# Weight loads, casts and subtractions pinned to TensorE's order of use, and plain groups that multiply all high parts before the low parts

## The chip, the cores and the metric

The kernel runs on one core of a Trainium2 chip. The metric is the device time of one execution in microseconds, from the start of the program to its end. The time before is a median of three runs. Where a profile is quoted, it is of one profiled execution, and every time in it is counted from the first instruction of the span.

## The reference

One decoder layer on a sequence of 256 tokens, width 2048, all in float32: a SwiGLU half-step, a mixer (dilated attention beside gated linear attention), cross-attention into 256 memory tokens, and a second SwiGLU half-step. The change touches the two half-steps most:

```
def swiglu(h, w_gate, w_up, w_down):
    return (jax.nn.silu(h @ w_gate) * (h @ w_up)) @ w_down

x = x + 0.5 * swiglu(rms_norm(x, ffn1_norm), ffn1_w_gate, ffn1_w_up, ffn1_w_down)
x = x + hybrid_mixer(rms_norm(x, mix_norm), ...)
x = x + cross_attention(rms_norm(x, xattn_norm), ...)
x = x + 0.5 * swiglu(rms_norm(x, ffn2_norm), ffn2_w_gate, ffn2_w_up, ffn2_w_down)
```

`w_gate` and `w_up` are 2048 x 5632, `w_down` is 5632 x 2048; each half-step reads all three from HBM once.

## The kernel before

**Numbers in two parts.** TensorE multiplies in float32r, a shortened float32. To keep the accuracy every operand is split into a high part (`h`, the operand cast to float32r) and a low part (`l`, the rest): for a weight, ScalarE casts (`wh`, L136), VectorE subtracts (`wl`, L137). A product is then three matmuls: high by high, low of x by high of w, high of x by low of w.

**Tiles and loads.** A weight load is one DMA on SP's queue of 128 x 2048 values (1 MB), in tiles `raw`. In the half-steps there are six buffers for `raw`, three for `wh` and three for `wl`. A buffer is written again when its last reader is done: a `wh` or `wl` buffer when TensorE has finished its last matmul on it.

**A half-step.** The 5632 columns are eleven column blocks f of 512, in three parts (f 0 to 3, 4 to 7, 8 to 10). After each part its blocks go through `w_down`. Block 0 is done plainly (`proj`). From then on each f is one call of `strassen` for `w_gate` and `w_up` together, here called a pair; there are 10 in each half-step, 20 in all. A pair multiplies the first two groups of 512 rows by seven products, P1 to P7 (L194, 12 matmuls each), in place of eight, and the other two groups plainly, for gate and for up: G1 (gate, group 2), then P7, then G2 (up, group 2), G3 (gate, group 3), G4 (up, group 3), 24 matmuls each by `mm3` (L163 to L165). A matmul has 128 x 128 of x as stationary operand and 512 columns of weights moving.

**What stands around the products.** The four loads of a pair are `ral`, `rar`, `rbr`, `rbl`. P1 uses `ral`; then VectorE adds `rar` into `ral` (L212) for P2, and then `rbr` into `ral` (L212) for P3. POOL issues two DMAs that accumulate: `rbr` into `rar` for P5, and `rbl` into `ral` for P7 (L216). P1, P3, P5, P7, G1 and G3 write the PSUM tile `x`, P2 writes `y`. ScalarE copies P1's result from `x` to `c0l` (L228) before P3 writes `x` on, and `y` to `ys` (L234). VectorE makes `c0r = ys - x` after P3 (L238) and `c1r = ys - x` after P5 (L243); P5 and G1 write `x` on after these. At the end of a pair ScalarE makes `sg` of the gate (L377) and VectorE `h` (L385); `h` is transposed on TensorE after the next pair's P2 (L355), and split again (`hTh`, `hTl`, L274 and L275).

**What sets the order.** A scheduler orders each engine's instructions when the kernel is built, by priorities and by its own model of when operands are ready; weight loads, casts and subtractions have a raised priority. Each engine, SP's queue too, then works through its list in that order. On all engines, TensorE too, instructions can so stand in another order than they are written.

Of the kernel before, what the change touches and what calls it, by code (L numbers as in the profile page):

```python
# [8 lines left out]
F32 = mybir.dt.float32  # L9
# [9 lines left out]
TT = S // P  # L19
# [30 lines left out]
def layer_kernel(ctx: ExitStack, tc: tile.TileContext, A: dict, out: bass.AP):  # L50
    nc = tc.nc
    V, SC, G, PE, SY = nc.vector, nc.scalar, nc.gpsimd, nc.tensor, nc.sync
# [21 lines left out]
    def FT(tag, bufs, shape, dt, name):  # L74
        return phase["pool"].tile(shape, dt, tag=tag, name=name, bufs=bufs)

    def W2(shape, name, dt=F32):
        return sp.tile(shape, dt, tag="w", name=name)
# [4 lines left out]
    def PM(shape, name):  # L83
        return pm.tile(shape, F32, tag="ps", name=name)
# [7 lines left out]
    def tick():  # L92
        due = []
        for e in pend:
            e[0] -= 1
            if e[0] <= 0:
                due.append(e)
        for e in due:
            pend.remove(e)
            e[1]()  # L100


    gain = con.tile([P, 82], F32, name="gain")

    xload, wload = [], []
    open_phase("half1", True)
    with tc.high_priority(100000):
        SY.dma_start(gain, A["gains"])
        for g in range(3):
            raw = wp.tile([P, 4, 512], F32, tag="raw", name="raw")  # L110
# [10 lines left out]
    def load(W, c, g):  # L121

        if wload:
            return wload.pop(0)
        kn, n = W.shape[-2:]
        with tc.high_priority(WPRI):
            phase["loads"] += 1
            if phase["half_step"] and phase["loads"] % 2:
                raw = FT("raw", FRAW, [P, kn, n], F32, "raw")
            else:  # L130
                raw = wp.tile([P, kn, n], F32, tag="raw", name="raw")
            SY.dma_start(raw, W[c, g])
        return raw

    def split(wh, wl, src):
        SC.copy(wh, src)  # L136
        V.tensor_sub(wl, src, wh.bitcast(F32))  # L137

    def wgroup(W, c, g, fine=None):

        raw = load(W, c, g)
        n = W.shape[-1]
        kn = W.shape[-2]
        whole = phase["half_step"]
        m = kn if whole else kn // 2
        for h in range(1 if whole else 2):
            with tc.high_priority(WPRI):
                wh, wl = (FT(x, FWB if whole else WB, [P, m, n], F32R, x) for x in ("wh", "wl"))
                for i in range(m if fine else 1):
                    d = slice(i, i + 1) if fine else slice(0, m)  # L150
                    if fine:
                        fine(m * h + i)
                    split(wh[:, d], wl[:, d], raw[:, m * h + d.start:m * h + d.stop])
            ks = [(kn * g + m * h + kk, wh[:, kk], wl[:, kk]) for kk in range(m)]
            for i in range(0, m, kn // 2):
                yield ks[i:i + kn // 2]

    def mm3(acc, lhs, half, first, last, ts=range(TT), seeded=False):

        for t in ts:  # L160
            for i, (k, wh, wl) in enumerate(half):
                lh, ll = lhs(k, t)
                PE.matmul(acc[t], lh, wh, start=first and i == 0, stop=False, skip_group_check=seeded)  # L163
                PE.matmul(acc[t], lh, wl, start=False, stop=False, skip_group_check=seeded)  # L164
                PE.matmul(acc[t], ll, wh, start=False, stop=last and i == len(half) - 1, skip_group_check=seeded)  # L165

# [4 lines left out]
    def sums_of(ga, gb, put):  # L173

        (ah, al), (bh, bl) = ga, gb
        fa, fb = (FT("h", 8, [P, 4, S], F32, n) for n in ("fa", "fb"))
        V.tensor_add(fa, ah.bitcast(F32), al.bitcast(F32))
        V.tensor_add(fb, bh.bitcast(F32), bl.bitcast(F32))
        t0, t1 = slice(0, P), slice(P, S)
        sa, sb = (FT("h", 8, [P, 2, 4, P], F32, n) for n in ("sa", "sb"))  # L180
        V.tensor_sub(sa[:, 0], fa[:, :, t1], fb[:, :, t1])
        V.tensor_sub(sa[:, 1], sa[:, 0], fa[:, :, t0])
        V.tensor_sub(sb[:, 0], fa[:, :, t0], fa[:, :, t1])
        V.tensor_add(sb[:, 1], fb[:, :, t0], sa[:, 1])
        for i, x in enumerate((sa, sb)):
            split(*put(i), x)

    def product(acc, lhs, w, start):

        wh, wl = w  # L190
        first = start
        for i, j, w in ((0, 0, wh), (1, 0, wh), (0, 1, wl)):
            for k in range(4):
                PE.matmul(acc, lhs(k)[i], w[:, k], start=first, stop=j == 1 and k == 3, skip_group_check=not start)  # L194
                first = False
        tick()

    def strassen(Wl, cl, Wr, cr, lhs, ab, sums, groups):

        a, b = ab  # L200
        ral, rar = load(Wl, cl, a), load(Wr, cr, a)
        rbr, rbl = load(Wr, cr, b), load(Wl, cl, b)

        def parts(src):
            with tc.high_priority(WPRI):
                wh, wl = (FT(x, FWB, [P, 4, 512], F32R, x) for x in ("wh", "wl"))
                split(wh, wl, src)
            return wh, wl

        def add(dst, x, y):  # L210
            with tc.high_priority(WPRI):
                V.tensor_add(dst, x, y)  # L212

        def accumulate(dst, x):
            with tc.high_priority(WPRI):
                G.dma_start(dst, x, accum_op=ALU.add)  # L216

        def of(g, t):
            return lambda k: lhs(4 * g + k, t)

        def s_(i):
            return lambda k: tuple(x[:, i, k] for x in sums)

        x, y = PM([P, 512], "x"), PM([P, 512], "y")
        c0l, c0r, c1r = (pa.tile([P, 512], F32, tag="acc", name="acc") for _ in range(3))
        product(x, of(a, 0), parts(ral), True)
        with tc.high_priority(WPRI):
            SC.copy(c0l, x)  # L228
        add(ral, ral, rar)
        accumulate(rar, rbr)  # L230
        product(y, s_(0), parts(ral), True)
        with tc.high_priority(WPRI):
            ys = W2([P, 512], "ys")
            SC.copy(ys, y)  # L234
        add(ral, ral, rbr)
        product(x, s_(1), parts(ral), False)
        with tc.high_priority(WPRI):
            V.tensor_sub(c0r, ys, x)  # L238
        product(c0l, of(b, 0), parts(rbl), False)
        accumulate(ral, rbl)  # L240
        product(x, s_(2), parts(rar), False)
        with tc.high_priority(WPRI):
            V.tensor_sub(c1r, ys, x)  # L243
        product(c0r, s_(3), parts(rbr), False)
        accs = ((c0l, x), (c0r, c1r))
        for i, g in enumerate(groups):
            for acc, W, c in zip(accs, (Wl, Wr), (cl, cr)):
                for h, half in enumerate(wgroup(W, c, g)):
                    mm3(acc, lhs, half, False, i == len(groups) - 1 and h == 1, seeded=True)
                    tick()  # L250
                if i == 0 and W is Wl and c == cl:
                    product(x, of(b, 1), parts(ral), False)
        return accs

    def proj(W, c, lhs, groups, fine=None, last=False):

        n = W.shape[-1]
        acc = [pa.tile([P, n], F32, tag="acc", name="acc") for _ in range(TT)]
        groups = list(groups)
        for i, g in enumerate(groups):  # L260
            if fine and i:
                fine(4 * i)
            if last and i == len(groups) - 1:
                both = [w for half in wgroup(W, c, g) for w in half]
                for t in range(TT):
                    mm3(acc, lhs, both, i == 0, True, (t,))
                break
            for h, half in enumerate(wgroup(W, c, g, fine if i == 0 else None)):
                mm3(acc, lhs, half, i == 0 and h == 0, i == len(groups) - 1 and h == 1)
                tick()  # L270
        return acc
# [376 lines left out]
    for p2 in range(2):  # L648
        acc = proj(win, 8 + p2, lhs_x, range(4))
# [18 lines left out]
    for p2 in range(2):  # L668
        acc = proj(win, 10 + p2, lhs_x, range(4))
# [183 lines left out]
    acc = proj(A["xattn_w_k"], 0, lhs_mem, range(4))  # L853
# [6 lines left out]
    for c in range(NC):  # L860
        acc = proj(A["w_out"], c, lhs_m, (2, 3, 0, 1))
# [7 lines left out]
    acc = proj(A["xattn_w_q"], 0, lhs_x, range(4))  # L869
# [49 lines left out]
    for hv in range(2):  # L919
        acc = proj(A["xattn_w_v"], hv, lhs_mem, range(2))  # L920
# [7 lines left out]
    for c in range(0, NC, 2):  # L928
        pair = (c, c + 1)
        acc = {d: [pa.tile([P, 512], F32, tag="acc", name="acc") for _ in range(TT)] for d in pair}  # L930
# [104 lines left out]
```

## Time and profile before

| | |
|---|---|
| median of 3 runs | 1958.37 us (1956.77 to 1959.21) |
| the profiled execution | 1957.9 us |
| its span, first to last instruction | 1956.1 us |
| TensorE (PE) busy | 1924.5 us |
| VectorE (DVE) busy | 1270.5 us |
| ScalarE (ACT) busy | 988.7 us |
| read from HBM | 370.72 MB |

The profile names an instruction by engine, line and tiles (`wl<-raw,wh`: written from). A row of a timeline has the start, the time from the first start to the last end of equal instructions in a row, and in brackets how long the engine stood idle before and what it waited for. Matmuls overlap: one lasts 0.39 us in the profile, while the next starts long before that. The granted clock is the share of TensorE's full 2.4 GHz; its lower level, 0.5, is 1.2 GHz.

### The profile page before, as it was taken

How to read it: one execution, taken by the hardware profiler on the slowest of the kernel's cores; microseconds unless marked ns; L12 is line 12 of the kernel's file. 1: busy time of each engine (PE TensorE's matmuls, PEld its weight loads, DVE VectorE, ACT ScalarE, POOL GpSimd, SP SyncE). 2: the span in 40 equal slices, each digit the busy share in tenths (PEclk: the TensorE clock that was granted, in tenths of full speed). 3: DMA queues.
4: the chain of work that ended last, by engine and by line, in shares of the span. 5: the costliest groups of instructions: out<-in, count | busy, mean ns of one | idle time of the engine just before them, and what ended most of it. 6: DMA issues, size and time to landing. Idle time of an engine off the chain costs nothing.

```text
span 1956.1 us, 21465 instructions
## 1 busy us (share of the span) xinstructions
PE 1924.5 (98%) x8760; PEld 1586.4 (81%) x8760; DVE 1270.5 (65%) x1027; ACT 988.7 (51%) x956; POOL 96.1 (5%) x101
## 2 busy tenths in 40 slices
PE   8999999999999999999999999899999999999999
PEld 6888878888878888778888889688887788887887
DVE  6776467775578655546785566777646777457863
ACT  6555345553356446444675446555534555335642
POOL 2000000000000000002230000000000000000000
PEclk9999999999999999999999999999999999999999
DMA  9677547775567725445465554567755777556771
GB/s 368 235 236 258 190 148 264 271 268 192 173 220 237 281 82 186 156 167 191 172 232 207 183 192 151 217 236 233 260 184 146 252 272 274 203 178 215 237 285 59
DMA packets 63294, 416.14 MB, mean 213 GB/s; under 512 B 7099, under 2 KB 8251, under 8 KB 14428
## 3 DMA queue, kind: packets, MB, share of 16 engines
q1 hardware_dynamic: 56284, 370.74, 49.9%
q0 software_dynamic: 5760, 41.95, 10.4%
q10 hardware_dynamic: 1152, 2.10, 0.3%
q8 instruction: 68, 1.11, 0.2%
q14 instruction: 30, 0.25, 0.0%
HBM read 370.72 MB, written 2.10 MB: 191 GB/s over the span
## 4 chain that ended last, share of the span: by engine, by line
PE 74%; DVE 15%; ACT 5%; issue 4%; DMA 1%; POOL 0%; SPq 0%; ACTq 0%; DVEq 0%
PE acc L164 21%; PE acc L165 20%; PE acc L163 20%; DVE wl L137 10%; ACT wh L136 5%; PE x L194 4%; DVE raw L212 4%; PE x L165 1%; PE x L164 1%; PE acc L194 1%; PE x L163 1%; DVE h L385 1%; DMA xr<-in_xT_dram 1%; DVE acc L238 1%; PE y L194 0%
## 5 line engine op out<-in xcount | busy, mean ns | idle before, releaser
L137 DVE TENSOR_TENSOR wl<-raw,wh 128x2048 fp32r<-128x2048 f32 (+2 forms) x487 | 931.5, 1932 | 582.6 <-ACT wh L136 581.8
L136 ACT CAST wh<-raw 128x2048 fp32r<-128x2048 f32 (+2 forms) x487 | 777.0, 1619 | 692.5 <-PE acc L165 503.9
L163 PE MATMUL acc<-wh,xTh 128*128 128x512 f32 x1024 | 402.3, 394 | 16.3 <-ACT wh L136 16.3
L164 PE MATMUL acc<-wl,xTh 128*128 128x512 f32 x1024 | 402.9, 393 | 8.9 <-DVE wl L137 8.9
L165 PE MATMUL acc<-wh,xTl 128*128 128x512 f32 x1024 | 400.5, 391 | 0.0
L163 PE MATMUL acc<-wh,hTh 128*128 128x512 f32 x704 | 274.7, 390 | 0.0
L165 PE MATMUL acc<-wh,hTl 128*128 128x512 f32 x704 | 274.0, 389 | 0.0
L164 PE MATMUL acc<-wl,hTh 128*128 128x512 f32 x704 | 273.9, 389 | 0.0
L163 PEld LDWEIGHTS acc<-wh,xTh 128*128 128x128 f32 x1024 | 192.4, 189 | 59.5 <-ACT wh L136 18.9
L164 PEld LDWEIGHTS acc<-wl,xTh 128*128 128x128 f32 x1024 | 193.3, 189 | 56.9 <-DVE wl L137 17.7
L165 PEld LDWEIGHTS acc<-wh,xTl 128*128 128x128 f32 x1024 | 193.4, 189 | 39.7
L165 PEld LDWEIGHTS acc<-wh,hTl 128*128 128x128 f32 x704 | 132.2, 188 | 27.4
L164 PEld LDWEIGHTS acc<-wl,hTh 128*128 128x128 f32 x704 | 132.2, 188 | 27.2
L163 PEld LDWEIGHTS acc<-wh,hTh 128*128 128x128 f32 x704 | 132.2, 188 | 27.1
L216 POOL DMA_DIRECT2D raw<-raw x40 | 34.6, 864 | 1179.5 <-DVE raw L212 966.9
L212 DVE TENSOR_TENSOR raw<-raw 128x2048 f32<-128x2048 f32 x40 | 91.5, 2288 | 0.7
L165 PE MATMUL x<-wh,xTl 128*128 128x512 f32 x160 | 62.6, 391 | 0.0
L164 PE MATMUL x<-wl,xTh 128*128 128x512 f32 x160 | 62.5, 391 | 0.0
L163 PE MATMUL x<-wh,xTh 128*128 128x512 f32 x160 | 62.4, 390 | 0.0
L228 ACT COPY acc<-x 128x512 f32<-128x512 f32 x20 | 11.4, 571 | 95.6 <-PE x L194 95.6
L396 DVE SCALAR_TENSOR_TENSOR x<-acc,x 128x512 f32<-128x512 f32 x48 | 33.0, 687 | 31.6 <-PE acc L165 31.6
L163 PE MATMUL acc<-wh,mTh 128*128 128x512 f32 x128 | 50.1, 392 | 0.0
(302 smaller groups left out, 1958.9 us busy)
## 6 DMA issues: line engine op xcount, KB each, us to landing
raw<-in_ffn_w_up_dram SPq DMA_DIRECT2D x88, 1024.0 KB, 7.0
raw<-in_ffn_w_down_dram SPq DMA_DIRECT2D x88, 1024.0 KB, 4.9
raw<-in_ffn_w_gate_dram SPq DMA_DIRECT2D x85, 1024.0 KB, 6.9
raw<-in_w_in_dram SPq DMA_DIRECT2D x48, 1024.0 KB, 4.7
raw<-raw POOLq DMA_DIRECT2D x40, 1024.0 KB, 6.9
raw<-in_w_out_dram SPq DMA_DIRECT2D x16, 1024.0 KB, 4.7
raw<-in_xattn_w_k_dram SPq DMA_DIRECT2D x4, 1024.0 KB, 4.8
raw<-in_xattn_w_q_dram SPq DMA_DIRECT2D x4, 1024.0 KB, 5.0
```

Source lines behind the costliest of these rows:

```text
L136: SC.copy(wh, src)
L137: V.tensor_sub(wl, src, wh.bitcast(F32))
L163: PE.matmul(acc[t], lh, wh, start=first and i == 0, stop=False, skip_group_check=seeded)
L164: PE.matmul(acc[t], lh, wl, start=False, stop=False, skip_group_check=seeded)
L165: PE.matmul(acc[t], ll, wh, start=False, stop=last and i == len(half) - 1, skip_group_check=seeded)
L194: PE.matmul(acc, lhs(k)[i], w[:, k], start=first, stop=j == 1 and k == 3, skip_group_check=not start)
L212: V.tensor_add(dst, x, y)
L216: G.dma_start(dst, x, accum_op=ALU.add)
L228: SC.copy(c0l, x)
L238: V.tensor_sub(c0r, ys, x)
L385: V.scalar_tensor_tensor(h, upv[t], r[:, t:t + 1], sg[t], op0=ALU.mult, op1=ALU.mult)
L396: V.scalar_tensor_tensor(xs[c][:, t], acc[t], 0.5, xs[c][:, t], op0=ALU.mult, op1=ALU.add)
```

## The change

`in_turn` ties each weight load to the load written before it, each weight cast to the cast before it, and each weight subtraction to the subtraction before it, so that on its queue none can pass another. The splits of the activations (`sums_of`, `split_from_psum`) are not tied. `whole` takes the place of `mm3` for the plain groups of a pair: first high by high for both halves of the rows (8 matmuls), then low of x by high of w (8), then high of x by low of w (8). The number of matmuls, loads, casts and subtractions stays. `tick`, which lets the transposes in, is called as often as before.

```
+    def in_turn(key, ins):
+        if key in issued:
+            tc.add_manual_dep(ins.ins, issued[key], ...NoSync..., reason="weights in turn")
+        issued[key] = ins.ins.name
...
-            SY.dma_start(raw, W[c, g])
+            in_turn("load", SY.dma_start(raw, W[c, g]))
...
     def split(wh, wl, src):
-        SC.copy(wh, src)
-        V.tensor_sub(wl, src, wh.bitcast(F32))
+        return SC.copy(wh, src), V.tensor_sub(wl, src, wh.bitcast(F32))
+
+    def wsplit(wh, wl, src):
+        for key, ins in zip(("cast", "sub"), split(wh, wl, src)):
+            in_turn(key, ins)
...
+    def whole(acc, lhs, group, last):
+        for i, j in ((0, 0), (1, 0), (0, 1)):
+            for t in range(TT):
+                for n, w in enumerate(group):
+                    PE.matmul(acc[t], lhs(w[0], t)[i], w[1 + j], start=False,
+                              stop=last and j == 1 and n == len(group) - 1, skip_group_check=True)
+            if i or j:
+                tick()
...
-                for h, half in enumerate(wgroup(W, c, g)):
-                    mm3(acc, lhs, half, False, i == len(groups) - 1 and h == 1, seeded=True)
-                    tick()
+                both = [w for half in wgroup(W, c, g) for w in half]
+                whole(acc, lhs, both, i == len(groups) - 1)
```

On TensorE the order differs in the 20 runs of G1 to G4 and nowhere else. Here is G1 of the pair that opens the second part of FFN2, before; its `wh` is number 10686, G2's is 10732:

```order
L194 MATMUL acc_10577<-wl_10669,sh_9204 128x512 x4
L163 MATMUL acc_10576<-wh_10686,xTh2_8932 128x512
L163 MATMUL x_10574<-wh_10686,xTh2_8932 128x512
L163 MATMUL acc_10577<-wh_10732,xTh2_8932 128x512
L163 MATMUL acc_10578<-wh_10732,xTh2_8932 128x512
L164 MATMUL acc_10576<-wl_10687,xTh2_8932 128x512
L165 MATMUL acc_10576<-wh_10686,xTl2_8933 128x512
```

The same place after:

```order
L216 MATMUL acc_10577<-wl_10669,sh_9204 128x512 x4
L184 MATMUL acc_10576<-wh_10686,xTh2_8932 128x512 x4
L184 MATMUL x_10574<-wh_10686,xTh2_8932 128x512 x4
L184 MATMUL acc_10576<-wh_10686,xTl2_8933 128x512 x4
L184 MATMUL x_10574<-wh_10686,xTl2_8933 128x512 x4
L184 MATMUL acc_10576<-wl_10687,xTh2_8932 128x512 x4
L184 MATMUL x_10574<-wl_10687,xTh2_8932 128x512 x4
L216 MATMUL x_10574<-wh_10714,xTh1_8820 128x512 x4
```

Two matmuls of G2 stood in G1 and are gone from there; `wl` is used after 16 matmuls in place of two to four.

ScalarE's list in a pair in the middle of a part, from P1's cast (9511) on, before (P2's is 9530, P3's 9565, P4's 9582, P5's 9599, P6's 9616, G1's 9634):

```order
L136 CAST wh_9511<-raw_9498 128x2048
L377 ACTIVATE sg_9490<-acc_9230,r4_8906 128x512
L377 ACTIVATE sg_9492<-x_9228,r4_8906 128x512
L136 CAST wh_9530<-raw_9498 128x2048
L228 COPY acc_9508<-x_9506 128x512
L136 CAST wh_9565<-raw_9498 128x2048
L136 CAST wh_9582<-raw_9504 128x2048
L234 COPY ys_9562<-y_9507 128x512
L136 CAST wh_9599<-raw_9500 128x2048
L136 CAST wh_9616<-raw_9502 128x2048
L136 CAST wh_9634<-raw_9632 128x2048
L274 CAST hTh_9546<-tp_9548 128x4x128
```

And after:

```order
L145 CAST wh_9511<-raw_9498 128x2048
L398 ACTIVATE sg_9490<-acc_9230,r4_8906 128x512
L145 CAST wh_9530<-raw_9498 128x2048
L398 ACTIVATE sg_9492<-x_9228,r4_8906 128x512
L145 CAST wh_9565<-raw_9498 128x2048
L145 CAST wh_9582<-raw_9504 128x2048
L250 COPY acc_9508<-x_9506 128x512
L145 CAST wh_9599<-raw_9500 128x2048
L256 COPY ys_9562<-y_9507 128x512
L295 CAST hTh_9546<-tp_9548 128x4x128
L295 CAST hTh_9546<-tp_9555 128x4x128
L145 CAST wh_9616<-raw_9502 128x2048
```

The copy of `c0l` went from ahead of P3's cast to behind P4's, the second `sg` behind P2's cast, and the casts of `hT` ahead of P6's. In 14 of the 20 pairs the list changes so. VectorE's list of the same 14 pairs changes too: the second addition (L212) goes ahead of the two `h`, `c0r` behind P5's subtraction, the two `hTl` to either side of P6's, and `c1r` behind G1's.

SP's queue in the pair of the first example, before (G1's load is 10684, G2's 10730, G3's 10760, G4's 10790; the next pair's `ral`, `rar`, `rbr`, `rbl` are 10828, 10830, 10832, 10834):

```order
L132 DMA raw_10730<-in_ffn2_w_up_dram 128x2048
L132 DMA raw_10790<-in_ffn2_w_up_dram 128x2048
L132 DMA raw_10760<-in_ffn2_w_gate_dram 128x2048
L132 DMA raw_10830<-in_ffn2_w_up_dram 128x2048
L132 DMA raw_10828<-in_ffn2_w_gate_dram 128x2048
L132 DMA raw_10834<-in_ffn2_w_gate_dram 128x2048
L132 DMA raw_10832<-in_ffn2_w_up_dram 128x2048
```

And after:

```order
L141 DMA raw_10730<-in_ffn2_w_up_dram 128x2048
L141 DMA raw_10760<-in_ffn2_w_gate_dram 128x2048
L141 DMA raw_10790<-in_ffn2_w_up_dram 128x2048
L141 DMA raw_10828<-in_ffn2_w_gate_dram 128x2048
L141 DMA raw_10830<-in_ffn2_w_up_dram 128x2048
L141 DMA raw_10832<-in_ffn2_w_up_dram 128x2048
L141 DMA raw_10834<-in_ffn2_w_gate_dram 128x2048
```

G3's load went ahead of G4's, and the next pair's four stand in the order in which they are used. At the start of FFN2 the first six loads stand as 8984, 9044, 9110, 8914, 9014, 9080 before and as 8914, 8984, 9014, 9044, 9080, 9110, the order of use, after.

## Rows read from the trace of the kernel before

**Rows 1.** Page, part 1: engine, busy us, share of the span, instructions.

```profile
PE 1924.5 (98%) x8760; PEld 1586.4 (81%) x8760; DVE 1270.5 (65%) x1027; ACT 988.7 (51%) x956; POOL 96.1 (5%) x101
```

**Rows 2.** Timeline of TensorE: start, us, what; pair at 1325, P1 to G1.

```profile
1325.40 1.07 PE L194 MATMUL x<-wh,xTh 128*128 128x512 f32 x4
...
1330.85 1.03 PE L355 MATMUL tp<-ident,h 128*128 128x128 f32 x8
1331.64 1.17 PE L194 MATMUL x<-wh,sh 128*128 128x512 f32 x4
...
1333.55 1.16 PE L194 MATMUL x<-wl,sh 128*128 128x512 f32 x4
...
1342.94 0.39 PE L163 MATMUL x<-wh,xTh 128*128 128x512 f32 x1
1343.52 0.50 PE L164 MATMUL acc<-wl,xTh 128*128 128x512 f32 x1 [0.19 <-DVE wl L137]
1343.86 0.40 PE L165 MATMUL acc<-wh,xTl 128*128 128x512 f32 x1
```

**Rows 3.** Waits of TensorE: us in total, times, longest us.

```profile
PE acc L163 <- ACT wh L136: 16.3, 7, 4.4
PE acc L164 <- DVE wl L137: 8.9, 18, 3.8
```

**Rows 4.** Timeline of TensorE: G1 of the four pairs that open a part.

```profile
293.92 0.73 PE L163 MATMUL acc<-wh,xTh 128*128 128x512 f32 x2 [2.43 <-ACT wh L136]
...
551.64 0.74 PE L163 MATMUL acc<-wh,xTh 128*128 128x512 f32 x2 [1.59 <-ACT wh L136]
...
1517.48 0.89 PE L163 MATMUL acc<-wh,xTh 128*128 128x512 f32 x2 [2.42 <-ACT wh L136]
...
1776.69 0.50 PE L163 MATMUL acc<-wh,xTh 128*128 128x512 f32 x1 [1.50 <-ACT wh L136]
```

**Rows 5.** Timeline of ScalarE: P7's and G2's casts, pair at 1498.

```profile
1513.72 3.71 ACT L136 CAST wh<-raw 128x2048 fp32r<-128x2048 f32 x2 [2.76 <-PE acc L194]
```

**Rows 6.** Page, part 6: the accumulating DMAs; KB each, us to landing.

```profile
raw<-raw POOLq DMA_DIRECT2D x40, 1024.0 KB, 6.9
```

**Rows 7.** Stretches: length, each engine's busy us (instructions), granted clock, DMA share, GB/s.

```profile
1517.60:1521.10 3.50, 3.50 (x9) 2.73 (x10) 2.56 (x2) 0.00 (x0) 0.00 (x0) 0.54 1.04 435
...
1325.40:1367.72 42.32, 42.13 (x190) 34.46 (x188) 32.80 (x20) 23.79 (x17) 1.70 (x2) 1.00 0.72 248
1497.92:1543.22 45.30, 42.88 (x181) 34.63 (x180) 31.58 (x18) 22.76 (x15) 1.71 (x2) 0.96 0.69 232
```

**Rows 8.** Timeline of ScalarE: P1's cast to P3's and P4's, pair at 1325.

```profile
1314.72 1.91 ACT L136 CAST wh<-raw 128x2048 fp32r<-128x2048 f32 x1 [4.43 <-PE acc L165]
1318.81 0.69 ACT L377 ACTIVATE sg<-acc,r 128x512 f32<-128x512 f32 x1 [2.17 <-PE acc L165]
...
1321.38 1.91 ACT L136 CAST wh<-raw 128x2048 fp32r<-128x2048 f32 x1 [0.52 <-DVE raw L212]
1328.32 0.57 ACT L228 COPY acc<-x 128x512 f32<-128x512 f32 x1 [5.04 <-PE x L194]
1329.22 3.72 ACT L136 CAST wh<-raw 128x2048 fp32r<-128x2048 f32 x2 [0.33 <-DVE raw L212]
```

**Rows 9.** Timeline of VectorE: `h`, second addition, P3's and P4's subtractions, same pair.

```profile
1325.53 1.40 DVE L385 SCALAR_TENSOR_TENSOR h<-acc,r,sg 128x512 f32<-128x512 f32 x2
1326.85 2.28 DVE L212 TENSOR_TENSOR raw<-raw 128x2048 f32<-128x2048 f32 x1
1331.17 4.49 DVE L137 TENSOR_TENSOR wl<-raw,wh 128x2048 fp32r<-128x2048 f32 x2 [2.04 <-ACT wh L136]
```

**Rows 10.** Timeline of SP's queue: two loads for FFN2's first block.

```profile
1219.12 10.00 SPq L132 DMA_DIRECT2D raw<-in_ffn_w_gate_dram  x2
```

**Rows 11.** Timeline of ScalarE: cast of FFN2's fourth weight group.

```profile
1245.24 1.91 ACT L136 CAST wh<-raw 128x2048 fp32r<-128x2048 f32 x1 [5.25 <-PE acc L165]
```

**Rows 12.** Timeline of TensorE: P3 of the first pair of FFN1.

```profile
65.32 1.20 PE L194 MATMUL x<-wh,sh 128*128 128x512 f32 x4 [0.67 <-ACT acc L228]
```

More of the change, by code (lines that the diff above doesn't have):

```diff
@@ L100, in tick @@
             e[1]()
+    issued = {}
+    def in_turn(key, ins):
+        if key in issued:
+            tc.add_manual_dep(ins.ins, issued[key], mybir.DependencyInfo(
+                mybir.DependencyClass.NoSync, mybir.DependencyReason.DATA), reason="weights in turn")
+        issued[key] = ins.ins.name
     gain = con.tile([P, 82], F32, name="gain")
@@ L152, in wgroup @@
                         fine(m * h + i)
-                    split(wh[:, d], wl[:, d], raw[:, m * h + d.start:m * h + d.stop])
+                    wsplit(wh[:, d], wl[:, d], raw[:, m * h + d.start:m * h + d.stop])
             ks = [(kn * g + m * h + kk, wh[:, kk], wl[:, kk]) for kk in range(m)]
@@ L206, in parts @@
                 wh, wl = (FT(x, FWB, [P, 4, 512], F32R, x) for x in ("wh", "wl"))
-                split(wh, wl, src)
+                wsplit(wh, wl, src)
             return wh, wl
```

## Prediction

> **What bounds the kernel now.** I read the page's busy table first, then TensorE's timeline and its waits, and last the queues that feed the places where it stands still. The reader is to see that TensorE is busy for 98% of the span [rows 1], so nothing that moves other engines can give more than the little that TensorE waits or runs slowly. At full speed a 512-column matmul starts every 227 ns: the 24 of the first two products take 1330.85 - 1325.40 = 5.45 us [rows 2]. The span of 1956.1 us less its busy time leaves 31.6 us. Of these 25.2 us are waits for weights: 16.3 us for a cast (`wh`) and 8.9 us for a subtraction (`wl`) [rows 3]. Part of these lie where the change does nothing: the start of the kernel, and one wait of 3.8 us for `wl` at the start of FFN2 [rows 3], which ends behind eleven vector operations whose order stays.
>
> What is left lies in the 20 pairs (calls of `strassen`), always at the same matmul: the first plain group, G1. Two kinds:
>
> - In the four pairs that open the second and third part of each FFN, TensorE stops for 2.43, 1.59, 2.42 and 1.50 us for a cast [rows 4]. The cast is not G1's own. The order on TensorE takes two matmuls of G2 in between, so G1 waits for G2's cast, which stands on ScalarE behind P7's, and that one runs only at 1513.72 [rows 5], when the second accumulating DMA has landed (6.9 us after its issue [rows 6]).
> - In the other pairs (15 of 16; the sixteenth opens FFN1) it stops two matmuls into G1, for G1's own `wl` [rows 2].
>
> **The sum, part by part.** Durations are of the profiled execution, 1957.9 us, 0.5 us under the median of the runs.
>
> *Part starts.* The bracket of a row counts from the modelled end of the matmul before; from start to start it is 0.16 us more (1343.52 - 1342.94 - 0.227 = 0.35 where the bracket says 0.19 [rows 2]). So 2.43 + 1.59 + 2.42 + 1.50 + 4 x 0.16 = 8.6 us. The first matmuls after a stop run late too, 0.11 us for the next one (1343.86 - 1343.52 - 0.227 [rows 2]), 0.15 in all: 4 x 0.15 = 0.6 us. After the stop at 1517.48 the granted clock is at its lower level: 0.54 on average over 3.5 us [rows 7] (1.2 GHz in place of 2.4 for most of it), which costs 3.5 x 0.46 = 1.6 us. Together 10.8 us. As a check, that pair takes 45.30 us and a plain one with eight more transposes 42.32 [rows 7].
>
> *The other pairs.* 0.35 + 0.15 = 0.50 us at G1, and at P3, whose `wl` is also just late, 1.16 instead of 1.07 us for four matmuls [rows 2]: 0.09. 15 x 0.59 = 8.9 us.
>
> *Does the change remove them?* On TensorE only G1 to G4 are reordered. G1 is now 16 matmuls on `wh` and then 8 on `wl`, and no matmul of G2 stands in it. At a part start G2's cast is then needed 34 matmuls (7.7 us) later than now; it was late by 2.4. P7's own cast follows the DMA at 1513.72 and its subtraction about 4.2 us later, at 1518; G1 began two matmuls ahead of the stop, at 1517.48 - 2.43 - 0.39 - 0.23 = 1514.43 [rows 4], so P7 would start 24 matmuls later, at 1519.9, and need `wl` 1.8 us after that. So nothing takes the place of the stop. In the other pairs `wl` is needed 16 x 0.227 = 3.6 us into G1 instead of 0.45, against 0.35 us of lateness. Both hold with the queues as they are; but the change also pins loads, casts and subtractions, which moves the queues of ScalarE and VectorE in 14 pairs. Those I lay out by hand, with P1's first matmul as zero (1325.40 in the trace).
>
> *Before:* P1's cast -10.7 [rows 8], P2's -4.0 [rows 8], second addition (`ral` + `rbr`) 1.45 to 3.73 [rows 9], copy of `c0l` 2.9 and P3's cast 3.8 [rows 8], P3's subtraction 5.8 [rows 9], P3 on TensorE 6.24 [rows 2].
>
> *After:* a `wh` buffer is free 8 matmuls (1.8 us) earlier, since the last 8 of a group read `wl` alone. P1 takes the buffer of the group G2 before it, which ends at -10.9, so its cast can start at -12.5 and end at -10.6; its subtraction (2.25 us each in a row, [rows 9]) waits for the `wl` buffer until about -10.7 as now, and ends at -8.3; the first addition ends at -6.0. ScalarE then has one `sg` in front (0.69 [rows 8], ready when 20 of G3's 24 matmuls are done, -6.15, so until -5.5), P2's cast until -3.6, P2's subtraction until -1.3, and the second addition, no longer behind the two `h` (1.40 [rows 9]), until 1.0. P3's cast 1.1 to 3.0, P4's until 4.8 (1.81 more, from 3.72 for two [rows 8]), and only then the copy of `c0l` (0.57 [rows 8]) until 5.4. P3 overwrites what that copy reads, so P3 waits for it, but P3 is due at 6.24: **0.8 us of slack**. P3's, P4's and P5's subtractions end at 5.3, 7.5 and 9.8; the difference `c0r`, now behind P5's, ends at 10.5, and P5 is due when P4 ends, 11.7: **1.2 us**. P6's and G1's subtractions and the two `hTl` come before the difference `c1r`, which ends at 16.4; TensorE needs it at the fifth matmul of G1, 18.0: **1.6 us**. G1's `wl` ends at 15.8 and is needed at 20.7. I cost these moves at nothing: what hides them is P1 and P2, 5.4 us of TensorE work. If that cover is too short each late microsecond comes 14 times; the bounds are 0 and 27 us (the second rival).
>
> *Loads.* On SP's queue G3's load now goes before G4's, and the next pair's four in order of use. G3's buffer is free when P6's subtraction ends (13.0), so it is issued near 13.5 and lands near 18.5, while its cast waits for a `wh` buffer until 20.9: 2 us of slack in ScalarE, 12 before TensorE needs it. At the start of FFN2 two loads (`raw_9044`, `raw_9110`) now stand behind one whose buffer is freed at 1228.8 (the second of the two that span 1219.12 to 1229.12 [rows 10]). They land about 12 us later than that at the latest, near 1241, and the fourth group, the first to use them, is cast at 1245.24, when the first group frees a `wh` [rows 11]. The price is 0; its bounds are -1 us (the first load of FFN2 goes 18 us earlier) and +2 us.
>
> Sum: 10.8 + 8.9 = 19.7 us. 1957.9 - 19.7 = 1938.2 for a profiled run, and 1958.4 - 19.7 = **1938.7 us** for the median.
>
> **Rivals.**
>
> *The cover is a little short (13%).* P3's `c0l` copy or P5's `c0r` difference ends later than laid out, by the 0.8 to 1.2 us of slack plus 0.3 to 1: a sum of ten durations with handovers that I took at 0.03 to 0.2 us can be off by that. 14 x 0.3 to 1.0 = 4 to 14 us of the 19.7 go back: 1943 to 1953. For it: the order on VectorE leaves no free time between 3.0 and 16.4. Against it: three separate slacks, each several handovers wide.
>
> *The copy behind the cast makes it slower (5%).* If the second addition does not move forward but ends at 3.73 as in the trace, P3's cast runs 3.8 to 5.7, P4's to 7.5, the copy to 8.1, and P3 starts 1.95 us late, 14 times: 27.3 us against 19.7, so 1958.4 + 7.6 = 1966 us. It decides at the point where the second addition ends later than 1.8 (6.24 less 0.6, 3.7 and a handover). For it the trace has a case: in the first pair of FFN1 the copy comes late and P3 waits 0.67 us for it by the bracket [rows 12]. Against it: the addition is freed of two `h` and of the late `wh` buffer, 2.7 us in all, by buffers and order and not by chance. PSUM — Partial Sum Buffer of the Trainium skill, section "Engine vs sequencer instructions", has the rule that speaks against this change: the queues of ScalarE and VectorE are strict FIFO, so a copy that is ready at 2.9 cannot pass a cast in front of it. By that rule the copy ends at 5.4 or at 8.1 according to the addition alone; if a ready copy could pass, the sum of 19.7 would stand without the slack at P3. The trace agrees with the rule, by that wait of 0.67 us.
>
> *It does not do what it says (5%).* If the stops had another cause than the order (a load or the accumulating DMA late in itself), they would reappear at G3 or P7: about 1956 to 1960 us. Against it: the brackets name casts and subtractions, not DMAs, on TensorE [rows 3, 4].
>
> *More than laid out (5%).* The pinned order could also spare the 0.8 us at the first pair and some of FFN2's start: 1934.
>
> **How the numbers follow.** The forecast, 1935 to 1942 (the runs shown spread by 2.4 us, and 0.1 us of error in a term of 15 pairs is 1.5), has 72%. With the 5% below it and about half of the 13% above it, the range 1934 to 1948 holds a little over 8 in 10. A measurement of this kernel tells 0.2% (4 us) from no change. Faster: 72 + 13 + 5 = 90%; same: 5%; slower: 5%.
>
> **What would show it.** Right: no cast or subtraction in front of any plain group's first matmuls; pairs near 41.7 us, and 41.0 at part starts; full clock near 1518; the second addition ending about 1 us after P1 starts. Wrong: P3 waiting for the copy of `c0l` (L228 before) or P5 for `c0r`; a stop at G3 behind a load; FFN2's first groups waiting for a load.

## The result, and the profile after

The changed kernel takes 1939.29 us (median; 1938.24 to 1940.05), the kernel before took 1957.74 us beside it: a ratio of 0.9905, 95% interval 0.9888 to 0.9922, so 15 to 22 us less. The forecast was 1938.7 us.

Part 1 of the page after (engine, busy us, share of the span, instructions; it answers to [rows 1]):

```profile
span 1938.2 us, 21492 instructions
...
PE 1917.5 (99%) x8760; PEld 1588.9 (82%) x8760; DVE 1273.2 (66%) x1027; ACT 989.7 (51%) x956; POOL 96.6 (5%) x101
```

TensorE's busy time falls by 7 us although it does the same 8760 instructions: a matmul counts as busy longer where it runs late (0.50 us in place of 0.39 [rows 2]) or at the lower clock (0.89 us for two that at full clock take 0.73 [rows 4]). The idle time falls from 31.6 to 20.7 us. TensorE's waits after (us in total, times, longest us; they answer to [rows 3]):

```profile
PE acc L175 <- ACT wh L145: 8.6, 4, 4.4
PE acc L176 <- DVE wl L145: 5.6, 3, 3.3
PE wps L451 <- DVE mhalf L445: 1.1, 1, 1.1
PE x L216 <- ACT acc L250: 0.7, 1, 0.7
```

No plain group of a pair (L184 now) is in this list any more. What is left on `wh` and `wl` is L175 to L177 (`mm3`, outside the pairs): the start of the kernel, 0.4 us at 723.7, and the start of FFN2, where the change removed no wait. The 0.7 us is the first pair's wait for `c0l` [rows 12], also as before.

The stretches of the pairs (length, busy us of PE, PEld, DVE, ACT and POOL, granted clock, DMA share, GB/s; they answer to [rows 7]), and G1 of the pair that opens FFN2's second part in TensorE's timeline (it answers to [rows 4]):

```profile
1317.78:1359.47 41.69, 41.69 (x190) 34.61 (x188) 32.97 (x20) 23.87 (x17) 1.71 (x2) 1.00 0.73 252
1489.11:1530.10 40.99, 40.99 (x182) 33.58 (x181) 33.10 (x19) 22.64 (x15) 1.71 (x2) 1.00 0.79 266
```

```profile
1504.71 1.07 PE L216 MATMUL acc<-wl,sh 128*128 128x512 f32 x4
1505.62 1.07 PE L184 MATMUL acc<-wh,xTh 128*128 128x512 f32 x4
1506.52 1.07 PE L184 MATMUL x<-wh,xTh 128*128 128x512 f32 x4
1507.43 1.07 PE L184 MATMUL acc<-wh,xTl 128*128 128x512 f32 x4
```

The middle pair goes from 42.32 to 41.69 us, the part-start pair from 45.30 to 40.99; no row has a bracket, the clock is full, and four matmuls take 0.91 us from start to start, which is full speed. TensorE is busy in both from end to end: there is nothing left in them for an order to give.

Now the queues that the prediction laid out by hand, in the same middle pair (P1 begins at 1317.78). ScalarE, then VectorE, then P3, P5 and G1's fifth matmul on TensorE:

```profile
1318.88 3.72 ACT L145 CAST wh<-raw 128x2048 fp32r<-128x2048 f32 x2 [4.18 <-DVE raw L234]
1322.50 0.59 ACT L250 COPY acc<-x 128x512 f32<-128x512 f32 x1
...
1316.47 2.29 DVE L234 TENSOR_TENSOR raw<-raw 128x2048 f32<-128x2048 f32 x1
...
1327.43 0.69 DVE L260 TENSOR_TENSOR acc<-ys,x 128x512 f32<-128x512 f32 x1
...
1333.63 0.69 DVE L265 TENSOR_TENSOR acc<-ys,x 128x512 f32<-128x512 f32 x1
...
1324.01 1.17 PE L216 MATMUL x<-wh,sh 128*128 128x512 f32 x4
...
1329.55 1.07 PE L216 MATMUL x<-wh,sh 128*128 128x512 f32 x4
...
1335.89 1.07 PE L184 MATMUL x<-wh,xTh 128*128 128x512 f32 x4
```

| step, counted from P1 | laid out | measured | slack laid out | slack measured |
|---|---|---|---|---|
| second addition ends | 1.0 | 0.98 | | |
| copy of `c0l` ends; P3 at 6.23 | 5.4 | 5.31 | 0.8 | 0.92 |
| `c0r` ends; P5 at 11.77 | 10.5 | 10.34 | 1.2 | 1.43 |
| `c1r` ends; G1's fifth matmul at 18.11 | 16.4 | 16.54 | 1.6 | 1.57 |

### The profile page after: what moved, and what is told of

The parts are those of the page before. It is cut to its first block, busy times and chain, and to the rows that moved or that the text cites. A ratio compares the mean times of both kernels' runs of the same rounds, so it can differ in the third digit from the quotient of the medians.

```text
span 1938.2 us, 21492 instructions
## 1 busy us (share of the span) xinstructions
PE 1917.5 (99%) x8760; PEld 1588.9 (82%) x8760; DVE 1273.2 (66%) x1027; ACT 989.7 (51%) x956; POOL 96.6 (5%) x101
## 3 DMA queue, kind: packets, MB, share of 16 engines
q0 software_dynamic: 5760, 41.95, 10.5%
## 4 chain that ended last, share of the span: by engine, by line
PE 97%; DVE 1%; ACT 1%; DMA 0%; SPq 0%; issue 0%; POOL 0%; ACTq 0%; DVEq 0%
PE acc L176 17%; PE acc L177 17%; PE acc L175 17%; PE acc L184 17%; PE x L216 11%; PE acc L216 6%; PE x L184 6%; PE y L216 3%; PE tp L376 1%; DVE wl L145 1%; PE tp L336 0%; ACT wh L145 0%; DMA xr<-in_xT_dram 0%; PE dsp L635 0%; PE op L652 0%; PE op L656 0%
## 5 line engine op out<-in xcount | busy, mean ns | idle before, releaser
L175 PE MATMUL acc<-wh,hTh 128*128 128x512 f32 x704 | 274.7, 390 | 0.0
L177 PE MATMUL acc<-wh,hTl 128*128 128x512 f32 x704 | 274.0, 389 | 0.0
L175 PE MATMUL acc<-wh,xTh 128*128 128x512 f32 x544 | 216.6, 400 | 8.6 <-ACT wh L145 8.6
L176 PE MATMUL acc<-wl,xTh 128*128 128x512 f32 x544 | 214.1, 394 | 5.6 <-DVE wl L145 5.6
L177 PE MATMUL acc<-wh,xTl 128*128 128x512 f32 x544 | 213.6, 393 | 0.0
L177 PEld LDWEIGHTS acc<-wh,hTl 128*128 128x128 f32 x704 | 132.1, 188 | 27.4
L175 PEld LDWEIGHTS acc<-wh,hTh 128*128 128x128 f32 x704 | 132.2, 188 | 27.0
L175 PEld LDWEIGHTS acc<-wh,xTh 128*128 128x128 f32 x544 | 103.2, 191 | 32.0 <-ACT wh L145 10.2
L184 PE MATMUL acc<-wl,xTh 128*128 128x512 f32 x480 | 121.8, 389 | 0.0
L184 PE MATMUL acc<-wh,xTh 128*128 128x512 f32 x480 | 121.8, 389 | 0.0
L184 PE MATMUL acc<-wh,xTl 128*128 128x512 f32 x480 | 121.8, 389 | 0.0
L177 PEld LDWEIGHTS acc<-wh,xTl 128*128 128x128 f32 x544 | 103.2, 190 | 21.5
L184 PEld LDWEIGHTS acc<-wh,xTh 128*128 128x128 f32 x480 | 90.1, 188 | 18.7
L184 PEld LDWEIGHTS acc<-wl,xTh 128*128 128x128 f32 x480 | 90.1, 188 | 18.7
L184 PEld LDWEIGHTS acc<-wh,xTl 128*128 128x128 f32 x480 | 90.1, 188 | 18.7
```

What stands on the lines that cost most here:

```text
L184: PE.matmul(acc[t], lhs(w[0], t)[i], w[1 + j], start=False, stop=last and j == 1 and n == len(group) - 1, skip_group_check=True)
```

## The experiments

Two theories stood at the start. **Mine**: the gain is the order of the plain groups on TensorE; the ties cost and bring nothing. **Rivals**: the loads in the order of use carry part of it; the wh buffer that comes free earlier, and the new queues behind it, carry the middle pairs; the cover of the moved copy is thin and fails. The table gives the length of the pairs (first matmul of P1 to the first one behind G4, from the traces), and the median of each kernel. "Middle" are the 14 pairs whose queues the change moves, "part start" the four that open a part.

| kernel | middle | part starts | first of FFN1, FFN2 | median us |
|---|---|---|---|---|
| before | 42.27 to 42.32 | 43.73, 42.93, 45.30, 42.83 | 42.79, 42.29 | 1957.74 |
| after | 41.69 to 41.71 | 40.94 to 40.99 | 42.69, 41.81 | 1939.29 |
| whole_only | 41.69 to 41.71 | 40.93 to 41.03 | 42.68, 41.79 | 1939.86 |
| turn_only | 42.26 to 42.31 | 43.73, 42.87, 45.35, 42.83 | 42.79, 42.29 | 1958.01 |
| low_w_first | 41.75 to 41.83 | 40.95 to 40.98 | 42.68, 41.81 | 1939.77 |
| mm3_in_turn | 42.49 to 42.54 | 42.08 to 42.09 | 43.01, 42.52 | 1956.05 |
| d0 | 41.69 to 41.71 | 42.89 to 42.90 | 44.01, 43.89 | 1951.77 |
| d2 | 41.69 to 41.71 | 43.63 to 45.26 | 45.92, 44.69 | 1960.29 |
| d4 | 42.47 to 42.51 | 46.13 to 47.40 | 48.87, 47.34 | 1985.04 |
| low_w_copy_late | 43.57 to 43.59 | 42.90 to 44.51 | 44.01, 43.91 | 1979.87 |

### The two halves of the change, each alone

whole_only (the ties gone, the plain groups as after):

```
     def in_turn(key, ins):
-        if key in issued:
+        if False:
```

> The change without in_turn: loads, casts and subtractions are free again, the plain groups of a pair multiply high parts first. In the built program TensorE's order is that of the full change, ScalarE's and VectorE's lists differ from it only at the start of FFN2, and SP's queue is that of the kernel before (G4's load ahead of G3's). Theory (the gain is all in the order of the plain groups on TensorE, and in what that order does to the two cast queues): 1939 us, 1937 to 1942; pairs near 41.7 us and 41.0 at part starts. Rival (the order of the loads carries part of it): G3 waits for its cast behind a late load, and up to 10 us of the 19 are missing, 1945 to 1949 us.

Measured: 1939.86 us (1939.61 to 1940.62), ratio 0.9907 to before, interval 0.9891 to 0.9924. Waits of TensorE:

```profile
PE acc L175 <- ACT wh L145: 8.5, 4, 4.4
PE acc L176 <- DVE wl L145: 4.9, 3, 3.3
```

turn_only (the ties as after, the plain groups by `mm3`):

```
-                both = [w for half in wgroup(W, c, g) for w in half]
-                whole(acc, lhs, both, i == len(groups) - 1)
+                for h, half in enumerate(wgroup(W, c, g)):
+                    mm3(acc, lhs, half, False, i == len(groups) - 1 and h == 1, seeded=True)
+                    tick()
```

> The change without the new order of the plain groups: in_turn alone. In the built program TensorE's order is that of the kernel before, the cast queues differ from it only at the start of FFN2, SP's queue is that of the full change. Theory (all of the gain is in the plain groups): no change within the spread, 1956 to 1960 us; the stops of 2.4, 1.6, 2.4 and 1.5 us at the part starts and the late subtraction in the other pairs stay. Rival (loads in the order of use bring operands in time): the part-start stops shrink, 1947 to 1953 us.

Measured: 1958.01 us (1957.08 to 1959.98), ratio 1.0000, interval 0.9991 to 1.0009. Waits of TensorE:

```profile
PE acc L175 <- ACT wh L145: 15.5, 7, 3.5
PE acc L176 <- DVE wl L145: 9.1, 18, 3.8
```

What follows: the whole gain is in the plain groups' order, and the ties give nothing either way. The lists of the built programs say why: a program with the ties of the loads alone has the changed kernel's lists on every engine, so the ties of casts and subtractions move nothing more, and without any tie ScalarE's and VectorE's lists differ from the changed kernel's only at the start of FFN2. The moves in the queues of 14 pairs that the prediction put down to the ties are the scheduler's answer to the new order on TensorE.

The ties of the loads do change one wait, but not TensorE's. In whole_only G4's load stands ahead of G3's in all 20 pairs, as before (though 50 of the 388 entries of SP's queue are not where the kernel before has them). ScalarE then waits for loads of the gate's weights, in 16 of the 18 cases for G3's, 60.8 us in whole_only (first row) against 3.8 in the changed kernel (second row):

```profile
ACT wh L145 <- DMA raw<-in_ffn_w_gate_dram: 60.8, 18, 5.0
```

```profile
ACT wh L145 <- DMA raw<-in_ffn_w_gate_dram: 3.8, 4, 1.9
```

In the pair of whole_only that begins at 1317.34, ScalarE's cast for G3, and G3's first matmuls on TensorE:

```profile
1339.75 1.91 ACT L145 CAST wh<-raw 128x2048 fp32r<-128x2048 f32 x1 [3.99 <-DMA raw<-in_ffn_w_gate_dram]
...
1348.15 1.07 PE L184 MATMUL acc<-wh,xTh 128*128 128x512 f32 x4
```

The cast ends at 1341.66, 6.5 us before TensorE needs it. So the rival was right that G3's cast waits for a late load, and wrong that this reaches TensorE.

### What the new order consists of

low_w_first (high by high, then the low part of the weight, then the low part of x):

```
-        for i, j in ((0, 0), (1, 0), (0, 1)):
+        for i, j in ((0, 0), (0, 1), (1, 0)):
```

> The full change, but a plain group multiplies high by high, then high of x by low of w, then low of x by high of w: the weight's low part is used from the 9th matmul instead of the 17th, and wh is held to the end of the group. The built lists of ScalarE and VectorE are then in the middle pairs those of the kernel before (both sg ahead of P2's cast, copy of c0l ahead of P3's cast, second addition behind both h). Theory (what counts is that no low part is needed at once: 8 matmuls are 1.8 us against 0.35 us of lateness; at part starts that nothing of G2 stands in G1): all but the 0.09 us at P3 is kept, 1940.5 us, 1939 to 1943. Rival (the gain of the middle pairs came from the wh buffer that is free 8 matmuls earlier and the queues that follow from it): 0.5 us of each of 14 pairs comes back, about 1947 us.

Measured: 1939.77 us (1939.61 to 1942.41), ratio 0.9909, interval 0.9894 to 0.9924. Its middle pair, with P3's last matmuls (`x<-wl,sh`), and G1:

```profile
1325.01 1.15 PE L216 MATMUL x<-wl,sh 128*128 128x512 f32 x4
...
1335.08 1.07 PE L184 MATMUL x<-wh,xTh 128*128 128x512 f32 x4
1335.98 1.07 PE L184 MATMUL acc<-wl,xTh 128*128 128x512 f32 x4
```

G1 does not wait, with `wl` used after 8 matmuls. P3's `wl` is late by 0.08 us (1.15 where 1.07 is full speed), as it was before [rows 2], since here the second addition stands behind the two `h` again. So the 0.5 us at G1 came from the distance on TensorE alone, and the 0.08 at P3 from the `wh` buffer that is free earlier and the moved queues that follow from it: 41.78 to 41.70, in 14 pairs 1.1 us, too little to be told from the spread of the runs.

mm3_in_turn (turn_only, with the plain groups' matmuls tied as `mm3` writes them; the other engines' lists are those of turn_only):

```
+                row = [PE.matmul(...wh...), PE.matmul(...wl...), PE.matmul(...wh...)]
+                for ins in row if seeded else ():
+                    in_turn("mm", ins)
```

> in_turn alone, and besides the matmuls of the plain groups tied to each other as they are written, in threes (high by high, high by low of w, low by high): nothing of G2 can stand in G1, but the low part is needed by the second matmul. The lists of the other engines are those of the run with in_turn alone. Theory: at a part start G2's cast no longer stops G1, but G1's own wl does (subtraction to 1515.5 against a second matmul due at 1514.7 in the trace of before: 0.9 us plus 0.15); of 10.8 us 6.6 come. In the other pairs wl is needed one matmul earlier: 0.23 us more each, 15 times, 3.4 us. Sum 3.2 us faster than before: 1954.5 us, 1953 to 1957; part-start pairs 41.9 to 42.1 us, the others 42.5, clock full near 1518. Rival (the interleaved matmuls of G2 are the whole cause in all pairs): 1939 to 1942 us.

Measured: 1956.05 us (1955.04 to 1957.42), ratio 0.9989, interval 0.9980 to 0.9998. G1 of a middle pair (first row) and of the pair that opens FFN2's second part, in TensorE's timeline, and the latter pair's stretch:

```profile
1345.41 0.50 PE L176 MATMUL acc<-wl,xTh 128*128 128x512 f32 x1 [0.41 <-DVE wl L145]
...
1516.82 0.39 PE L175 MATMUL acc<-wh,xTh 128*128 128x512 f32 x1
1518.00 0.50 PE L176 MATMUL acc<-wl,xTh 128*128 128x512 f32 x1 [0.79 <-DVE wl L145]
1518.34 0.39 PE L177 MATMUL acc<-wh,xTl 128*128 128x512 f32 x1
```

```profile
1500.30:1542.38 42.08, 41.29 (x181) 33.50 (x180) 31.58 (x18) 22.77 (x15) 1.70 (x2) 1.00 0.73 250
```

This separates the two causes that the sum added up. Without G2's matmuls in G1 the stop of 2.42 us for a cast is gone and the clock stays full, but G1's own `wl` is then 0.79 us late, and 0.41 in the middle pairs, where it had been 0.19. Both parts were forecast, 42.08 and 42.5 us a pair. The interleaving by the scheduler was thus not foolish: it had put one more `wh` matmul of G1 ahead of the first `wl`, which saved 0.2 us a pair (42.5 against 42.3), and at part starts two of G2 besides, which cost the stop. Multiplying all high parts first gives the distance without borrowing from G2.

### How thick the cover of the moved copy is

In d0 the copies of `c0l` and `ys` are tied behind P4's cast in all 20 pairs; d2 and d4 have two and four idle copies of 128x256 values ahead of them. The edit of d4 (`range(0)` in d0, `range(2)` in d2):

```
+        w3, w4 = parts(ral), parts(rbl)
...
+            for _ in range(4):
+                in_turn("cast", SC.copy(idle, idle))
+            in_turn("cast", SC.copy(c0l, x))
+            in_turn("cast", SC.copy(ys, y))
```

> The full change, with the copies of c0l and ys tied in this order behind P4's cast and ahead of P5's, in all 20 pairs; the base for the two delayed kernels. Theory: the copy of c0l ends where it ends now in the 14 middle pairs (0.9 us before P3 begins); P5's cast starts about 1 us later than now, and c0r then ends at 11.1 against 11.7: still in time. 1939 to 1942 us. Rival (the cover is already used up): P5 waits for c0r in most pairs, 1945 to 1950 us.

Measured: 1951.77 us, ratio 0.9965, interval 0.9952 to 0.9978.

> As d0, with two idle copies of 128x256 values (about 0.38 us each) ahead of the copy of c0l in all pairs. Theory (queues strictly in order; slack of 0.9 us at P3, 0.6 at P5): the copy ends at 6.1 against 6.24, c0r at 11.8 against 11.7 plus a handover: 0 to 0.3 us a pair, 14 to 20 pairs, so 0 to 6 us over d0: 1939 to 1948. Rival (much more slack than laid out): the same time as d0.

Measured: 1960.29 us, ratio 1.0008, interval 0.9998 to 1.0018.

> As d0, with four idle copies (about 1.5 us) ahead of the copy of c0l. Theory: the copy ends at 6.85, P3 begins 0.6 to 0.7 us late, and P5 0.2 us more, in 14 pairs, fewer or less in the other 6: 10 to 17 us over d0, 1950 to 1958 us. Rival (a ready copy passes the casts, or the slack is above 1.5 us): the same time as d0.

Measured: 1985.04 us, ratio 1.0127, interval 1.0110 to 1.0143. A middle pair of d2 (P1 at 1330.49) and of d4 (P1 at 1346.70), ScalarE and then P3:

```profile
1335.22 0.84 ACT L259 COPY idle<-idle 128x256 f32<-128x256 f32 x2
1335.96 0.58 ACT L260 COPY acc<-x 128x512 f32<-128x512 f32 x1
...
1336.72 1.17 PE L218 MATMUL x<-wh,sh 128*128 128x512 f32 x4
```

```profile
1351.43 1.71 ACT L259 COPY idle<-idle 128x256 f32<-128x256 f32 x4
1353.05 0.58 ACT L260 COPY acc<-x 128x512 f32<-128x512 f32 x1
...
1353.68 1.19 PE L218 MATMUL x<-wh,sh 128*128 128x512 f32 x4 [0.50 <-ACT acc L260]
```

In the 14 middle pairs the theory holds to a tenth: in d2 the copy ends 0.74 us later than in the changed kernel, still 0.18 us before P3, and costs nothing (41.69 to 41.71), in d4 it ends 6.93 us into the pair where P3 was due at 6.23, P3 follows 0.05 us behind it, and the pair is 0.78 us longer. So the cover is 0.9 us, less 0.05 of handover. The totals missed, all three, by the other six pairs, which I had not laid out. There the changed kernel keeps the copy ahead of P3's cast, and with reason. A part start of d0, ScalarE and then P3:

```profile
1499.47 3.71 ACT L147 CAST wh<-raw 128x2048 fp32r<-128x2048 f32 x2 [5.24 <-DVE raw L236]
1503.09 0.57 ACT L260 COPY acc<-x 128x512 f32<-128x512 f32 x1
...
1503.71 0.50 PE L218 MATMUL x<-wh,sh 128*128 128x512 f32 x1 [1.78 <-ACT acc L260]
```

P1 began at 1496.33, and without transposes P3 is due 5.44 us later, at 1501.77; the second addition comes later too (ScalarE waits for it until 1499.47, 3.1 us into the pair), and P3 stops for 1.78 us by the bracket. Pairs add 11 us to d0 (four times 1.9, 1.3 and 2.1), the medians differ by 12. Of d4's 33 us over d0 the middle pairs are 14 x 0.78 = 11, as laid out (0.8 to 0.9 a pair); the six, of which little was expected, are the rest.

low_w_copy_late builds the second rival: low_w_first's order, so that the second addition is late, and the copy tied behind P4's cast.

```
+        for i, j in ((0, 0), (0, 1), (1, 0)):
...
+        w3, w4 = parts(ral), parts(rbl)
...
+            in_turn("cast", SC.copy(c0l, x))
```

> The plain groups as high by high, high by low of w, low by high, so that the second addition stands behind both h as in the kernel before, and the copy of c0l tied behind P4's cast: the second rival of the prediction, built on purpose. Theory (strict order on ScalarE): second addition until 3.7, P3's cast until 5.7, P4's until 7.5, copy until 8.1 against P3 due at 6.24: P3 1.95 us late in 14 pairs, 27 us over the forecast, 1963 to 1968 us, slower than the kernel before. Rival (the place of a 0.57 us copy costs no more than its own length): under 8 us over the full change, below 1948 us.

Measured: 1979.87 us, ratio 1.0106, interval 1.0091 to 1.0121, slower than before. A middle pair (P1 at 1340.51), VectorE's second addition, ScalarE, and P3:

```profile
1341.95 2.28 DVE L234 TENSOR_TENSOR raw<-raw 128x2048 f32<-128x2048 f32 x1
...
1344.34 3.70 ACT L145 CAST wh<-raw 128x2048 fp32r<-128x2048 f32 x2 [5.95 <-DVE raw L234]
1347.95 0.58 ACT L258 COPY acc<-x 128x512 f32<-128x512 f32 x1
...
1348.59 1.19 PE L216 MATMUL x<-wh,sh 128*128 128x512 f32 x4 [1.60 <-ACT acc L258]
```

The second addition ends at 3.72, the copy at 8.02, P3 begins at 8.08 in place of 6.23 (3.7, 8.1 and 8.2 were laid out), and the middle pairs are 1.79 us longer than low_w_first's (1.95 expected): 25 us. Six other pairs add 16, not counted beforehand. The copy could have run since P1 ended, 2.9 us into the pair [rows 8], and ScalarE stood idle from then until 3.8; yet it ran behind the two casts, and P3 stood 1.60 us for it. PSUM — Partial Sum Buffer of the Trainium skill, section "Engine vs sequencer instructions", has this as a rule: ScalarE's queue is strictly first in, first out. This trace agrees, by the 1.60 us. The place of a copy of 0.58 us in a queue thus costs 40 us: the second rival's mechanism and price are real; what kept it away is that the second addition moves forward with the same change.

### A version that beats both

What is left stands at the start of the kernel and at the start of FFN2, there 3.3 us for the first cast and 3.3 for the first `wl`. In front of that `wl` VectorE still makes the sums of the activations, which nobody needs for another 50 us. sums_after ties the sums behind the gate's four subtractions, and the split of the fourth block of x behind the first of these; without this second tie the built program puts that block in front of the first `wl` in the sums' place.

```
+        for ins in (V.tensor_add(fa, ...), V.tensor_add(fb, ...)):
+            tc.add_manual_dep(ins.ins, behind, ...NoSync...)
...
+                if (c, g0) == (3, 64):
+                    tc.add_manual_dep(ins.ins, issued["sub"], ...NoSync...)
...
+                    behind = issued["sub"]
```

> The full change once more, beside the next kernel on the same chip. All theories: 1938 to 1941 us.

Measured: 1939.61 us (1939.01 to 1940.09); ratio to before 0.9897, interval 0.9881 to 0.9914.

> The full change, and the sums of the activations (sums_of) tied behind the first four weight subtractions of each half-step, and at the start of FFN2 the fourth activation block behind the first weight subtraction. TensorE's, SP's and POOL's lists stay. Theory (the stop of 3.3 us at the start of FFN2, and 2.3 us of the start of FFN1, are vector operations that nobody needs yet, in front of the first subtractions): at FFN2 the first wl ends 2.3 to 2.7 us earlier, at FFN1 1.0 to 1.2 us of fa in front of the third wl go; 1939.3 - 3.5 = 1935.8 us, 1932 to 1938, the spread from how long TensorE stays at its lower clock after the stop. Rival (the loads or the casts are late there anyway): same time as the full change, 1938 to 1941.

Measured: 1935.75 us (1935.41 to 1936.29); ratio to before 0.9877, interval 0.9863 to 0.9892. Its median lies 3.9 us under that of after_again on the same chip, and the ranges do not overlap. TensorE at the start of FFN2 in after_again and in sums_after:

```profile
1224.85 1.22 PE L175 MATMUL acc<-wh,xTh 128*128 128x512 f32 x2 [3.29 <-ACT wh L145]
1229.41 0.79 PE L176 MATMUL acc<-wl,xTh 128*128 128x512 f32 x1 [3.34 <-DVE wl L145]
```

```profile
1224.19 0.73 PE L175 MATMUL acc<-wh,xTh 128*128 128x512 f32 x2 [2.68 <-ACT wh L145]
1226.52 0.79 PE L176 MATMUL acc<-wl,xTh 128*128 128x512 f32 x1 [1.59 <-DVE wl L145]
```

The first `wl` matmul comes 2.9 us earlier, a little more than the 2.3 to 2.7 expected, and the whole difference of the two profiled spans (1937.4 and 1934.5) is that. The 1.0 to 1.2 us expected at the start of FFN1 don't show: the first pair begins at 58.85 and 58.71. One profile of each can't settle it, since that start lies between 58.2 and 60.5 in the traces of kernels with the same lists up to there. That the medians differ by a microsecond more than the profiles is within what single executions of either kernel spread.

## Why the prediction was right

*Part starts, 10.8 us.* Measured 10.9: the four pairs go from 43.73, 42.93, 45.30 and 42.83 to 40.99, 40.94, 40.99 and 40.99. The step "no matmul of G2 stands in it" is shown by mm3_in_turn, which has that alone: stop for the cast and clock drop gone, `wl` late instead. The 1.6 us for the clock hang on one stop of the four: after the stop of 2.43 us at 293.92 [rows 4] that pair takes 43.73 us, and after the equally long one at 1517.48 the clock falls and the pair takes 45.30 (45.35 in turn_only). Why the clock fell after one of them alone is not shown. The bracket of [rows 5] names TensorE for P7's cast, where the prediction names the DMA. The DMA bears it out:

```profile
1505.86 0.85 POOL L216 DMA_DIRECT2D raw<-raw  x1 [10.66 <-DVE wl L137]
```

It landed 7.8 us after this start (6.9 is the median of all), at 1513.6, 0.1 us before the cast; and the `wh` buffer, one of three used in turn, had been P5's, which ended near 1511.9.

*The other pairs, 8.9 us.* Measured 8.8 over 15 pairs. The step that `wl` is needed 3.6 us into G1, against 0.35 us of lateness, is shown by low_w_first, where 1.8 us do as well.

*The moves in the queues, 0.* Right in size, by the table of slacks above and by the middle pairs of d2 and d4. Wrong in the cause: "the change also pins loads, casts and subtractions, which moves the queues of ScalarE and VectorE in 14 pairs". whole_only has the moved queues without a single tie. Had the prediction been asked for the ties alone, it would have given them work that they don't do.

*Loads, 0, bounds -1 and +2.* Right: turn_only makes no difference, and in whole_only the late load holds ScalarE alone. The profile of the changed kernel does lose 1.1 us at the start of FFN2, though not to loads. The pairs of FFN1 give 9.0 us, its first pair starts 0.73 us later (within the 58.2 to 60.5 of traces with the same lists up to there, so that is spread), and FFN2's first pair starts only 7.15 us earlier: 9.0 - 0.7 - 7.15 = 1.1. It is TensorE's clock in that execution, as below. So of 19.76 us saved in the pairs 17.9 arrive in the profiled span; the medians beside each other gave 18.4, and 20.4 in after_again's runs.

*The rivals.* "The cover is a little short" did not happen: d2 took 0.74 us of the cover without a cost. "The copy behind the cast" did not happen, but was rightly priced in the 14 pairs that it counted: 1.79 us a pair against 1.95. "It does not do what it says" is half true in a harmless way, for the ties. "More than laid out": the first pair kept its 0.7 us, and FFN2's start its stop.

## What to carry to other kernels

When an operand is made in two steps, first order the consumer so that everything that needs the first step alone comes first: 8 matmuls of distance covered what the ties on the producers had not. Before crediting a tie or a priority, build the change without it and compare the lists: a scheduler that fills queues by its own model moves the other engines when one engine's order changes, and those moves need a slack of their own. And pin a step only where its slack has been laid out for each kind of loop body: the same copy was free in 14 pairs and cost 1.9 us in each of four others.

## What the runs showed of the hardware

At the start of FFN2 TensorE stops twice, for the first cast and for the first `wl`, and in every trace its granted clock is at the lower level (1.2 GHz of 2.4) around the second stop. That stretch in the kernel before (first row) and after (second), and in sums_after (third):

```profile
1234.60:1241.40 6.80, 3.02 (x8) 2.24 (x8) 6.80 (x6) 5.38 (x5) 0.00 (x0) 0.50 0.35 123
```

```profile
1225.20:1235.40 10.20, 6.23 (x14) 4.50 (x15) 10.20 (x10) 6.79 (x6) 0.00 (x0) 0.50 1.00 406
```

```profile
1225.30:1232.00 6.70, 5.48 (x13) 4.32 (x14) 6.70 (x7) 3.67 (x4) 0.00 (x0) 0.50 1.02 428
```

In the kernel before, the clock fell 0.6 us after the end of the first stop (1234.02); in the changed kernel it fell 0.6 us before that end (1225.83), and in sums_after 1.1 us behind it (1224.19). What costs time is the part behind the second stop, where TensorE works without a gap at half its speed: 2.8 us in the kernel before (from 1238.58), 5.0 in the changed kernel (from 1230.39), 5.5 in sums_after (from 1226.52). The 2.2 us between the first two cost half of that, which is the 1.1 us above. In the eleven traces without sums_after's ties this part goes from 2.8 to 6.0 us, and the time from FFN1's last pair to FFN2's first goes with it, from 622.7 to 624.2 us.

Neither the ties nor the plain groups decide it. With the changed kernel's lists at the start of FFN2 the lower level lasts 10.2 us in the changed kernel, 6.8 in turn_only and 10.2 in mm3_in_turn; with those of the kernel before, 6.8 there and 10.2 in whole_only. In all twelve traces it lasts 10.2 us where it begins at most 0.3 us behind the end of the first stop (seven traces), and 6.8 us where it begins 0.6 us or more behind it (five). What sets that moment is left open. So a difference of one microsecond between single profiles of these kernels is not to be credited to a change.
